# State-space decays from summed logs in a two-layer hybrid block, with their elementwise work moved off GpSimd

## The chip, the cores and the metric

The kernel runs on one core of one Trainium2 chip. The metric is the device time of one execution in microseconds (us); the number compared is the median of several runs. PE is the matrix engine (its weight loads are PEld), DVE the vector engine, ACT the scalar engine, POOL is GpSimd, SP issues the DMAs.

## The reference, cut to what matters

The whole program is a four-part model (two mixers and two expert layers) followed by a second model of two layers. Only the state-space part of those last two layers is touched. Per layer, 256 tokens in two chunks of 128, 32 heads of 64 channels in four groups of eight:

```python
def ssd_scan(xdt, la, bm, cm):          # la = dt * a, the log decay of each token and head
    ...
    def step(state, inp):
        xc, lac, bc, cc = inp
        acs = jnp.cumsum(lac, axis=1)
        seg = acs[:, :, None] - acs[:, None, :]
        lmat = jnp.where(mask, jnp.exp(jnp.where(mask, seg, 0.0)), 0.0)
        cb = jnp.einsum('bign,bjgn->bijg', cc, bc)
        y = jnp.einsum('bijgr,bjgrp->bigrp', cb[..., None] * lmat, xc)
        ...
ys = ys + d_skip * xs
ys = ys * silu(z)
ysg = ysg * rsqrt(mean(ysg * ysg) + EPS)    # one norm for each group of 512 channels
o_ssd = ys @ ssd_out
```

The decay between token j and token i of one head is the exponential of a difference of two running sums of `la`.

## The kernel before, in words

Each layer's matrix products are put in a list, the `Stream`. An item is one 512-column slab of a weight matrix, an item with 1024 rows takes four steps, and one step is one 128x2048 block of fp32 weights: `st.step()` issues the 24 products of a step in two halves of 12. Every weight is split into a high and a low fp32r part, ACT copying the high part (L293) and one engine subtracting it for the low part (L298); three products (L317) then give one fp32-like product. A step needs its own two blocks, split two steps ahead into one of three buffers. The low part runs on DVE, unless `self.on_pool` is 2: then every second one runs on POOL. An item ends with its evacuation: a convolution for the x channels (`conv`, ACT L1882, three DVE operations L1885, ACT L1886), a SiLU for the gate channels z (L1896), a sigmoid for the later gates (L1907).

The small stages are put between the steps by hand, in the order of the code. In `hybrid`, the retention part comes first; the state-space part begins with `st.through(n_ret)`. From there the list holds x0, z0, x1, z1, x2, z2, x3, z3 (four steps each), four gate items, the two slabs of `ssd_out` (eight steps each) and two of `w_o`: 72 steps.

For each group g and each half q (four heads), `decays` makes the matrices S0 (128x1024) and s1 (128x512): `logs` multiplies the causal mask `tri` with the high and the low part of the log decays, the high part on POOL and the low part on DVE (tile latri, L2019); `sums` multiplies these with a matrix of ones or with the strict mask (12 products of 512 columns, L2033), so that each sum of logs is made in the matrix engine; ACT takes exponentials from PSUM (L2039, L2042, L2044); DVE multiplies S0 by the masked scores cb (L2045) and POOL multiplies s1 (L2046). `prepare` runs this for group g+1 while group g is scanned: `tokens` transposes x (L2055) and weights it by dt (L2058), `scan` multiplies (L2069, L2072) and adds the skip (L2075), then ysT is multiplied by the gate (L2133), and `inv_rms` gives the norm: squares on ACT (L1760), two additions on POOL (L1761, L1763), a product with ones (L1767), a power on POOL (L274), a product that spreads it over partitions (L1753). `finish` applies it a group later (L2108, then split L305, L306). `inv_rms` also serves the four retention heads of a layer.

`tc.keep_in_program_order` (`keep`) pins an instruction behind everything written before it for its engine; what is not pinned is ordered by the compiler's own schedule. PSUM is eight banks: four for the stream's products (mm), four for all small stages (sml).

Of the kernel before, what the change touches and what calls it, by code (L numbers as in the profile page):

```python
# [10 lines left out]
F32 = mybir.dt.float32  # L11
F32R = mybir.dt.float32r
I32 = mybir.dt.int32
AF = mybir.ActivationFunctionType
OP = mybir.AluOpType
AX = mybir.AxisListType

T = 256
D = 1024
P = 128  # L20
# [127 lines left out]
class Model:  # L148
# [1607 lines left out]
    def inv_rms(self, yT, n, eps):  # L1756

        nc = self.nc
        sq = self.s("ir_q", [P, 4, T])
        nc.scalar.activation(sq, yT, AF.Square)  # L1760
        nc.gpsimd.tensor_tensor(sq[:, 0:2], sq[:, 0:2], sq[:, 2:4], op=OP.add)  # L1761
        s1 = self.s("ir_s", [P, T])
        nc.gpsimd.tensor_tensor(s1, sq[:, 0], sq[:, 1], op=OP.add)  # L1763
        yield
        pq = self.psum("sml")
        for t in range(2):
            ins = nc.tensor.matmul(pq[:, t:t + 1], s1[:, t * P:(t + 1) * P], self.ones[:, :1], start=t == 0, stop=t == 1)  # L1767
# [5 lines left out]
        pr = self.psum("sml")  # L1773
# [27 lines left out]
    def hybrid(self, l, cc, st, xT, consts=lambda: None):  # L1801
        nc, I = self.nc, self.I
        V, G, A, E = nc.vector, nc.gpsimd, nc.scalar, nc.tensor
        keep = self.tc.keep_in_program_order
# [170 lines left out]
        dtp, la, lar = next(dt)  # L1975
# [11 lines left out]
        tj = next(dt)  # L1987
# [25 lines left out]
        def logs(g, q, c):  # L2013

            h0 = g * 8 + q * 4
            out = []
            for part, eng in ((0, G), (1, V)):
                x_ = self.s("latri", [P, 4, P], F32R)
                eng.tensor_tensor(x_, tri.unsqueeze(1).to_broadcast([P, 4, P]),  # L2019
                                  lar[part][:, c, h0:h0 + 4].bitcast(F32).unsqueeze(2).to_broadcast([P, 4, P]), op=OP.mult)  # L2020
                out.append(x_)
            return out

        def decays(g, q, cb, s1):

            h0 = g * 8 + q * 4
            s0 = self.s("S0", [P, 4, T])
            lt = [logs(g, q, 0), logs(g, q, 1)]

            def sums(m, c, first=False):  # L2030
                p = self.psum("sml")
                for part in range(2):
                    ins = E.matmul(p, self.strict_ones[:, m], lt[c][part], start=part == 0, stop=part == 1)  # L2033
                    if first and part == 0:
                        keep(ins)
                return p
            yield
            p0 = sums(0, 0, True)
            A.activation(s0[:, :, 0:P], p0.rearrange("p (h i) -> p h i", h=4), AF.Exp)  # L2039
            p1 = sums(1, 1)  # L2040
            for j in range(4):
                A.activation(s0[:, j, P:T], p1[:, j * P:(j + 1) * P], AF.Exp, bias=tj[:, h0 + j:h0 + j + 1])  # L2042
            p2 = sums(0, 1)
            A.activation(s1[:, q], p2.rearrange("p (h i) -> p h i", h=4), AF.Exp)  # L2044
            V.tensor_tensor(s0, s0, cb[:, :T].unsqueeze(1).to_broadcast([P, 4, T]), op=OP.mult)  # L2045
            G.tensor_tensor(s1[:, q], s1[:, q], cb[:, T:].unsqueeze(1).to_broadcast([P, 4, P]), op=OP.mult)  # L2046
            yield s0
# [43 lines left out]
        self.on_pool = 2  # L2091
# [21 lines left out]
        for g in range(4):  # L2113
            st.step()
# [8 lines left out]
            st.step()  # L2123
# [4 lines left out]
            st.step()  # L2128
# [16 lines left out]
    def ssd_dt(self, l, cc, xT, sc):  # L2145
# [29 lines left out]
        lar = self.s("la_h", n, F32R), self.s("la_l", n, F32R)  # L2175
        self.split(*lar, la)
        yield dtp, la, lar
        pt = self.psum("sml")
        E.matmul(pt[:, :32], self.masks[:, 1, :], la[:, 0, :], start=True, stop=True)
        tj = self.s("tj", [P, 32])  # L2180
        V.tensor_copy(tj, pt[:, :32])
        yield tj
# [53 lines left out]
    def second_consts(self):  # L2236
# [5 lines left out]
        self.strict_ones = c.tile([P, 2, P], F32R, tag="late", name="strict_ones")  # L2242
        nc.scalar.activation(self.strict_ones[:, 0], self.masks[:, 1], AF.Copy)
        nc.scalar.activation(self.strict_ones[:, 1], self.ones, AF.Copy)
# [178 lines left out]
```

## Time and profile before

| | us |
|---|---|
| median of 3 runs | 2685.36 (2682.80 to 2686.85) |
| the profiled execution | 2682.83 |
| its span, first to last instruction | 2680.7 |
| state-space stage of layer 0, in the span | 1527 to 1692 |
| the same stage of layer 1 | 2220 to 2385 |
| PE busy | 2371.3, 88% of the span |
| DVE busy | 1260.7, 47% |
| ACT busy | 949.0, 35% |
| POOL busy | 492.3, 18% |

The stage of a layer is bounded here by the first product of masked scores (L2005) and the last spread of a norm (L1753). The busy shares are means over stages with different limits, so the stage's own rows count, not the page's.

### The profile page before, as it was taken

To read this page: it belongs to the slowest core of one execution; us is meant where nothing else is said; L and a number is where in the kernel's file an instruction comes from. 1 tells how busy PE (TensorE), PEld (TensorE's weight loads), DVE (VectorE), ACT (ScalarE), POOL (GpSimd) and SP (SyncE) were. 2 spreads that over 40 slices of the span, in tenths; PEclk is the share of its full clock that TensorE was granted. 3 is DMA by queue.
4 is the path that set the end of the run, shared out by engine and by line. 5 is a ranking of instruction groups with operands and counts; after the bars stand their busy time and mean duration, and the time that the engine had idled before them with its cause. 6 is when DMAs were issued, how large, how long until landed. Compare 5 with 4: busy or idle time off the path is not lost.

```text
span 2680.7 us, 40349 instructions
## 1 busy us (share of the span) xinstructions
PE 2371.3 (88%) x16773; PEld 1773.3 (66%) x16773; DVE 1260.7 (47%) x2067; ACT 949.0 (35%) x1565; POOL 492.3 (18%) x426
## 2 busy tenths in 40 slices
PE   8997777776879777777899998999999999899998
PEld 7862222222765222222789988999988999889997
DVE  5751133111863000000657677466556667855664
ACT  6431100001462000000445555454444556554543
POOL 1110001000320000000413165121122305621110
PEclk9998889999889989999999999999999999999999
DMA  5368999999249999999544533555555353344553
GB/s 187 104 258 355 373 421 421 421 421 381 103 137 388 421 421 421 421 422 411 205 167 142 173 127 111 173 173 180 178 180 173 132 184 126 111 157 173 183 188 141
DMA packets 208793, 660.97 MB, mean 247 GB/s; under 512 B 26554, under 2 KB 33116, under 8 KB 161500
## 3 DMA queue, kind: packets, MB, share of 16 engines
q1 hardware_dynamic: 202148, 657.23, 64.4%
q8 instruction: 135, 2.21, 0.3%
q10 hardware_dynamic: 6456, 1.08, 0.2%
q14 instruction: 54, 0.44, 0.0%
HBM read 657.22 MB, written 1.05 MB: 246 GB/s over the span
## 4 chain that ended last, share of the span: by engine, by line
PE 42%; DMA 16%; DVE 5%; POOL 3%; ACT 2%; SPq 1%; issue 1%; POOLq 0%; ACTq 0%; DVEq 0%
PE ps_mm L317 38%; DMA wx<-in_moe_w_down_dram 6%; DMA wx<-in_moe_w_up_dram 5%; DMA wx<-in_moe_w_gate_dram 4%; DVE whl L298 2%; ACT whl L293 1%; DVE cv L1885 1%; DVE latri L2019 1%; PE ps_sml L2069 1%; PE ps_sml L2033 1%; DMA w<-in_w_in_dram 1%; DVE yf L2108 1%; SPq L681 1%; PE ps_sml L1949 1%; POOL xn L1970 0%
## 5 line engine op out<-in xcount | busy, mean ns | idle before, releaser
L317 PE MATMUL ps_mm<-u,whl 128*128 128x256 f32 x8448 | 1058.6, 286 | 24.2 <-POOL whl L298 14.3
L317 PEld LDWEIGHTS ps_mm<-u,whl 128*128 128x128 f32 x8448 | 1035.8, 194 | 37.4 <-POOL whl L298 16.4
L298 DVE TENSOR_TENSOR whl<-w,whl 128x1024 fp32r<-128x1024 f32 x432 | 562.0, 1304 | 425.2 <-ACT whl L293 415.4
L293 ACT ACTIVATE whl<-w 128x1024 fp32r<-128x1024 f32 x472 | 497.1, 1058 | 510.0 <-PE ps_mm L317 479.0
L734 PE MATMUL ps_mm<-wx,xe 128*32 128x512 f32 x2048 | 369.6, 683 | 140.5 <-DMA wx<-in_moe_w_up_dram 93.7
L317 PE MATMUL ps_mm<-whl,u 128*128 128x512 f32 x1440 | 344.3, 396 | 4.8 <-ACT u L305 2.9
L734 PEld LDWEIGHTS ps_mm<-wx,xe 128*32 128x32 f32 x2048 | 81.4, 121 | 402.9 <-DMA wx<-in_moe_w_up_dram 173.2
L317 PEld LDWEIGHTS ps_mm<-whl,u 128*128 128x128 f32 x1440 | 269.6, 190 | 64.6 <-ACT u L305 3.9
L769 PE MATMUL ps_mm<-wx,hid 128*32 128x512 f32 x1024 | 215.8, 608 | 49.7 <-DMA wx<-in_moe_w_down_dram 38.7
L753 DVE TENSOR_TENSOR sl<-sl,ps_mm 128x512 f32<-128x512 f32 x16 | 11.0, 687 | 417.4 <-PE ps_mm L734 342.1
L769 PEld LDWEIGHTS ps_mm<-wx,hid 128*32 128x32 f32 x1024 | 50.8, 110 | 198.3 <-DMA wx<-in_moe_w_down_dram 91.9
L383 POOL TENSOR_TENSOR rstd<-rstd,mhalf 128x1 f32<-128x1 f32 x18 | 10.9, 617 | 795.4 <-DVE rstd L382 786.7
L298 POOL TENSOR_TENSOR whl<-w,whl 128x1024 fp32r<-128x1024 f32 x40 | 97.5, 2439 | 239.4 <-ACT whl L293 239.4
L773 DVE SCALAR_TENSOR_TENSOR y_lo<-ps_mm,sg,y_hi 128x512 fp32r<-128x512 f32 x32 | 24.0, 750 | 233.1 <-ACT y_hi L772 231.8
L760 ACT ACTIVATE hid<-ps_sml 128x512 f32<-128x512 f32 x16 | 9.6, 597 | 311.5 <-PE ps_sml L758 304.0
L772 ACT ACTIVATE y_hi<-ps_mm,sg 128x512 fp32r<-128x512 f32 x32 | 22.0, 688 | 212.4 <-PE ps_mm L769 212.3
L2214 POOL TENSOR_TENSOR yT<-yT,rb 128x256 f32<-128x256 f32 x44 | 40.9, 951 | 204.0 <-ACT yT L2213 204.0
L305 ACT ACTIVATE u<-yf 128x256 fp32r<-128x256 f32 x124 | 48.7, 413 | 72.8 <-DVE yf L2108 21.0
L1885 DVE SCALAR_TENSOR_TENSOR cv<-ps_mm,cols_cw,cv 128x253 f32<-128x253 f32 (+1 forms) x144 | 64.1, 475 | 19.6 <-ACT cv L1882 18.7
L752 ACT ACTIVATE sl<-ps_mm 128x512 f32<-128x512 f32 x16 | 9.6, 597 | 170.7 <-PE ps_mm L734 170.7
L306 DVE TENSOR_TENSOR u<-yf,u 128x256 fp32r<-128x256 f32 x124 | 60.2, 514 | 9.4 <-ACT u L305 9.4
L723 PE MATMUL ps_sml<-oh,u 128*128 128x128 f32 x512 | 62.1, 280 | 2.0 <-ACT u L532 2.0
(518 smaller groups left out, 2160.9 us busy)
## 6 DMA issues: line engine op xcount, KB each, us to landing
wx<-in_moe_w_gate_dram SPq DMA_DIRECT2D x128, 1024.0 KB
wx<-in_moe_w_up_dram SPq DMA_DIRECT2D x128, 1024.0 KB
wx<-in_moe_w_down_dram SPq DMA_DIRECT2D x128, 1024.0 KB
w<-in_w_in_dram SPq DMA_DIRECT2D x104, 1024.0 KB
w<-in_w_gate_up_dram SPq DMA_DIRECT2D x44, 1024.0 KB
w<-in_w_down_dram SPq DMA_DIRECT2D x20, 1024.0 KB
w<-in_ret_out_dram SPq DMA_DIRECT2D x16, 1024.0 KB
w<-in_ssd_out_dram SPq DMA_DIRECT2D x16, 1024.0 KB
```

The costliest lines, as they stand in the source:

```text
L293: ins = nc.scalar.activation(hi, src, AF.Copy)
L298: eng.tensor_tensor(lo, src, hi.bitcast(F32), op=OP.subtract)
L305: self.nc.scalar.activation(hi, src, AF.Copy)
L306: self.nc.vector.tensor_tensor(lo, src, hi.bitcast(F32), op=OP.subtract)
L317: ins = nc.tensor.matmul(out, a, b, start=start and i == 0, stop=stop and i == 2)
L681: nc.sync.dma_start(w, src)
L723: nc.tensor.matmul(pg[:, o:o + P], h[:, t, j, :], oh2[:, t, :], start=j == j0 and t == 0, stop=j == j0 + 3 and t == 1)
L734: nc.tensor.matmul(out[r, :], xe[:, k, r], w[k // 4][a][:, k % 4, :], start=k == 0, stop=k == NK - 1, tile_position=(0, a * SLOTS))
L769: nc.tensor.matmul(py[r, :], hid[:, m, r], wd(c, m, a), start=m == 0, stop=m == 3, tile_position=(0, a * SLOTS))
L1885: V.scalar_tensor_tensor(acc[:, s:], ps[:, :T - s], cw[i][:, b + m:b + m + 1], acc[:, s:], op0=OP.mult, op1=OP.add)
L1949: ins = E.matmul(py[:, o:o + T], v[0, h // 2][:, c0:c0 + P], sc[:, :T], start=b == b0, stop=False, skip_group_check=True)
L2214: nc.gpsimd.tensor_tensor(sil[s0][:, m, :], sil[s0][:, m, :], sc[1], op=OP.mult)
```

## The change

The log decays are summed once per layer, in `ssd_dt`: one product with the causal mask gives the running sums of all 64 columns, they are transposed, and kept as a high and a low row for each head in `rows`. In `decays`, four products per half (64 rows, 256 columns) select a head's row and spread it over all partitions; DVE subtracts the running sum of each partition and clips at zero (eight operations of 128x128 per half), and ACT takes the exponentials from SBUF, pinned to the program's order. The four masked-log products, `logs` and the two POOL multiplications are gone; the additions of `inv_rms` and the s1 product run on DVE; `on_pool` is no longer set in this stage. Three of the single steps in the group loop become two, so a group takes 11 steps instead of 8, and the norm of a group begins one step later after its squares.

```diff
     def inv_rms(self, yT, n, eps):
-        nc.gpsimd.tensor_tensor(sq[:, 0:2], sq[:, 0:2], sq[:, 2:4], op=OP.add)
+        nc.vector.tensor_tensor(sq[:, 0:2], sq[:, 0:2], sq[:, 2:4], op=OP.add)
         s1 = self.s("ir_s", [P, T])
-        nc.gpsimd.tensor_tensor(s1, sq[:, 0], sq[:, 1], op=OP.add)
+        nc.vector.tensor_tensor(s1, sq[:, 0], sq[:, 1], op=OP.add)
...
-        def logs(g, q, c):
...
         def decays(g, q, cb, s1):
             h0 = g * 8 + q * 4
             s0 = self.s("S0", [P, 4, T])
-            lt = [logs(g, q, 0), logs(g, q, 1)]
-
-            def sums(m, c, first=False):
...
+            banks = [self.psum("sml") for _ in range(2)]
+            along = [banks[j // 2][:, j % 2 * T:(j % 2 + 1) * T] for j in range(4)]
+            for j in range(4):
+                ins = E.matmul(along[j], self.heads[0:64, h0 + j:h0 + j + 1].to_broadcast([64, P]), rows, start=j % 2 == 0, stop=j % 2 == 1)
+                if j == 0:
+                    keep(ins)
+            for j in range(4):
+                for c, to in ((0, s0[:, j, 0:P]), (1, s1[:, q, j])):
+                    V.tensor_scalar(to, along[j][:, c * P:(c + 1) * P], sums[:, c, h0 + j:h0 + j + 1], 0.0, op0=OP.subtract, op1=OP.min)
             yield
-            p0 = sums(0, 0, True)
-            A.activation(s0[:, :, 0:P], p0.rearrange("p (h i) -> p h i", h=4), AF.Exp)
-            p1 = sums(1, 1)
             for j in range(4):
-                A.activation(s0[:, j, P:T], p1[:, j * P:(j + 1) * P], AF.Exp, bias=tj[:, h0 + j:h0 + j + 1])
-            p2 = sums(0, 1)
-            A.activation(s1[:, q], p2.rearrange("p (h i) -> p h i", h=4), AF.Exp)
+                keep(A.activation(s0[:, j, P:T], along[j][:, P:T], AF.Exp, bias=tj[:, h0 + j:h0 + j + 1]))
+            keep(A.activation(s0[:, :, 0:P], s0[:, :, 0:P], AF.Exp))
+            keep(A.activation(s1[:, q], s1[:, q], AF.Exp))
             V.tensor_tensor(s0, s0, cb[:, :T].unsqueeze(1).to_broadcast([P, 4, T]), op=OP.mult)
-            G.tensor_tensor(s1[:, q], s1[:, q], cb[:, T:].unsqueeze(1).to_broadcast([P, 4, P]), op=OP.mult)
+            V.tensor_tensor(s1[:, q], s1[:, q], cb[:, T:].unsqueeze(1).to_broadcast([P, 4, P]), op=OP.mult)
             yield s0
...
-        self.on_pool = 2
         pre = prepare(0)
...
         for g in range(4):
-            st.step()
+            st.step(2)
             if last:
                 finish(*last)
...
             ysT = self.u4([P, 4, T], "ys%d" % g)
-            st.step()
+            st.step(2)
             scan(g, 0, s0[0], s1, xdt, xs, ysT)
...
-            st.step()
+            st.step(2)
             scan(g, 1, s0[1], s1, xdt, xs, ysT)
...
     def ssd_dt(self, l, cc, xT, sc):
...
-        lar = self.s("la_h", n, F32R), self.s("la_l", n, F32R)
-        self.split(*lar, la)
-        yield dtp, la, lar
+        yield dtp
         pt = self.psum("sml")
-        E.matmul(pt[:, :32], self.masks[:, 1, :], la[:, 0, :], start=True, stop=True)
+        E.matmul(pt[:, :64], self.masks[:, 0, :], la.rearrange("p c h -> p (c h)"), start=True, stop=True, skip_group_check=True)
+        E.matmul(pt[:, 64:96], self.masks[:, 1, :], la[:, 0, :], start=False, stop=True, skip_group_check=True)
+        sums = self.s("la_sums", [P, 2, 2, 32])
+        for i in range(2):
+            V.tensor_copy(sums[:, :, i], pt[:, :64].rearrange("p (c h) -> p c h", c=2))
         tj = self.s("tj", [P, 32])
-        V.tensor_copy(tj, pt[:, :32])
-        yield tj
+        V.tensor_copy(tj, pt[:, 64:96])
+        pr = self.psum("sml")
+        for c in range(2):
+            E.transpose(pr[0:64, c * P:(c + 1) * P], sums[:, c].rearrange("p i h -> p (i h)"), self.ident)
+        rows = self.s("la_rows", [P, T], F32R)
+        high = self.s("la_high", [P, T], F32R)
+        A.activation(rows[0:32], pr[0:32, :T], AF.Copy)
+        A.activation(high[32:64], pr[32:64, :T], AF.Copy)
+        V.tensor_tensor(rows[32:64], pr[32:64, :T], high[32:64].bitcast(F32), op=OP.subtract)
+        yield sums[:, :, 0], rows[0:64], tj
```

## Rows read from the trace of the kernel before

**Rows 1.** The page's part 1: span, and busy time of each engine.
```profile
span 2680.7 us, 40349 instructions
PE 2371.3 (88%) x16773; PEld 1773.3 (66%) x16773; DVE 1260.7 (47%) x2067; ACT 949.0 (35%) x1565; POOL 492.3 (18%) x426
```

**Rows 2.** Table by stretch: us, busy of PE, PEld, DVE, ACT, POOL, clock, DMA.
```profile
1480.00:1527.00 47.00, 47.00 (x394) 47.00 (x393) 24.90 (x29) 22.73 (x32) 0.00 (x0) 1.00 0.55 187
...
1527.00:1692.00 165.00, 148.98 (x1149) 139.67 (x1148) 124.79 (x160) 94.43 (x166) 97.32 (x55) 0.97 0.35 119
2220.00:2385.00 165.00, 148.99 (x1149) 139.67 (x1148) 124.74 (x160) 94.44 (x166) 97.48 (x55) 0.97 0.35 119
```

**Rows 3.** PE's waits in 1527 to 1692: us in total, times, longest.
```profile
PE ps_mm L317 <- POOL whl L298: 7.2, 5, 1.6
PE ps_sml L2055 <- ACT u L1886: 6.5, 3, 2.4
PE ps_sml L2033 <- DVE latri L2019: 1.0, 2, 0.6
PE ps_sml L1753 <- POOL ir_r L274: 0.8, 1, 0.8
PE ps_sml L2033 <- POOL latri L2019: 0.4, 1, 0.4
```

**Rows 4.** PE in order of time, around one group's decays: start, duration, instruction.
```profile
1603.23 1.65 PE L2033 MATMUL ps_sml<-latri,strict_ones 128*128 128x512 f32 x6
1604.72 3.04 PE L317 MATMUL ps_mm<-u,whl 128*128 128x256 f32 x24
1607.59 1.53 PE L2033 MATMUL ps_sml<-latri,strict_ones 128*128 128x512 f32 x6
1608.96 5.92 PE L317 MATMUL ps_mm<-u,whl 128*128 128x256 f32 x48
1614.72 0.50 PE L1767 MATMUL ps_sml<-c_ones,ir_s 128*128 128x1 f32 x4
```

**Rows 5.** PE in order of time, the first products after three of the waits.
```profile
1578.16 4.39 PE L317 MATMUL ps_mm<-u,whl 128*128 128x256 f32 x22 [1.63 <-POOL whl L298]
...
1591.96 4.61 PE L317 MATMUL ps_mm<-u,whl 128*128 128x256 f32 x24
...
1668.22 4.12 PE L317 MATMUL ps_mm<-u,whl 128*128 128x256 f32 x24
```

**Rows 6.** Table by stretch again, one of those three places (columns of Rows 2).
```profile
1592.00:1597.00 5.00, 5.00 (x32) 4.73 (x31) 3.34 (x6) 2.42 (x6) 0.00 (x0) 0.66 0.37 137
```

**Rows 7.** DVE's groups by shape in 1527 to 1692: busy us, mean ns, idle before.
```profile
L298 DVE TENSOR_TENSOR whl<-w,whl 128x1024 fp32r<-128x1024 f32 x20 | 36.9, 1846 | 17.5 <-ACT whl L293 17.4
L2019 DVE TENSOR_TENSOR latri<-c_masks,la_l 128x512 fp32r<-128x512 f32 x16 | 21.8, 1398 | 0.0
L2045 DVE TENSOR_TENSOR S<-S,cbm 128x1024 f32<-128x1024 f32 x8 | 12.7, 1586 | 5.2 <-ACT S L2042 5.2
L2108 DVE SCALAR_TENSOR_TENSOR yf<-u,cols_b,ir_b 128x256 f32<-128x256 f32 x12 | 11.0, 938 | 0.0
L2133 DVE TENSOR_TENSOR u<-u,u 128x1024 f32<-128x1024 f32 x4 | 8.2, 2040 | 0.0
...
L2008 DVE TENSOR_TENSOR cbm<-ps_sml,c_masks 128x128 f32<-128x128 f32 x4 | 1.2, 292 | 0.7 <-PE ps_sml L2006 0.7
```

**Rows 8.** Single lines, ns min/median/max: L298 in 1480 to 1527, then L2019 and L2108, whole span.
```profile
L298 DVE TENSOR_TENSOR whl<-w,whl x17: 1210/1225/1227, 1479.8 to 1526.5; 128x1024 fp32r<-128x1024 f32 x17
...
L2019 DVE TENSOR_TENSOR latri<-c_masks,la_l x32: 745/1522/2826, 1529.0 to 2335.5; 128x512 fp32r<-128x512 f32 x32
...
L2108 DVE SCALAR_TENSOR_TENSOR yf<-u,cols_b,ir_b x32: 468/472/2601, 1587.1 to 2387.9; 128x256 f32<-128x256 f32 x32
```

**Rows 9.** ACT in order of time: first and last step of one convolution's evacuation (x1).
```profile
1574.19 0.60 ACT L1882 ACTIVATE cv<-ps_mm,cols_b,cols_cw 128x256 f32<-128x256 f32 x1
...
1590.97 0.42 ACT L1886 ACTIVATE u<-cv 128x256 f32<-128x256 f32 x1
```

More of the change, by code (lines that the diff above doesn't have):

```diff
@@ L1974, in hybrid @@
         st.through(n_v - 1)
-        dtp, la, lar = next(dt)
+        dtp = next(dt)
         sc = scores(0)
@@ L1986, in hybrid @@
         sc = scores(1)
-        tj = next(dt)
+        sums, rows, tj = next(dt)
         for h in range(4):
@@ L2011, in masked @@
             return cb
-        def logs(g, q, c):
[L2015 to L2022, printed above, removed]
         def decays(g, q, cb, s1):
@@ L2027, in decays @@
             s0 = self.s("S0", [P, 4, T])
-            lt = [logs(g, q, 0), logs(g, q, 1)]
-            def sums(m, c, first=False):
[L2031 to L2036, printed above, removed]
+            banks = [self.psum("sml") for _ in range(2)]
[7 more added lines that the diff above has]
+                    V.tensor_scalar(to, along[j][:, c * P:(c + 1) * P], sums[:, c, h0 + j:h0 + j + 1], 0.0, op0=OP.subtract, op1=OP.min)
             yield
-            p0 = sums(0, 0, True)
-            A.activation(s0[:, :, 0:P], p0.rearrange("p (h i) -> p h i", h=4), AF.Exp)
-            p1 = sums(1, 1)
             for j in range(4):
-                A.activation(s0[:, j, P:T], p1[:, j * P:(j + 1) * P], AF.Exp, bias=tj[:, h0 + j:h0 + j + 1])
-            p2 = sums(0, 1)
-            A.activation(s1[:, q], p2.rearrange("p (h i) -> p h i", h=4), AF.Exp)
+                keep(A.activation(s0[:, j, P:T], along[j][:, P:T], AF.Exp, bias=tj[:, h0 + j:h0 + j + 1]))
+            keep(A.activation(s0[:, :, 0:P], s0[:, :, 0:P], AF.Exp))
+            keep(A.activation(s1[:, q], s1[:, q], AF.Exp))
             V.tensor_tensor(s0, s0, cb[:, :T].unsqueeze(1).to_broadcast([P, 4, T]), op=OP.mult)
-            G.tensor_tensor(s1[:, q], s1[:, q], cb[:, T:].unsqueeze(1).to_broadcast([P, 4, P]), op=OP.mult)
+            V.tensor_tensor(s1[:, q], s1[:, q], cb[:, T:].unsqueeze(1).to_broadcast([P, 4, P]), op=OP.mult)
             yield s0
@@ L2241, in second_consts @@
         self.retm = self.retm.rearrange("p (h t) -> p h t", h=4)
-        self.strict_ones = c.tile([P, 2, P], F32R, tag="late", name="strict_ones")
-        nc.scalar.activation(self.strict_ones[:, 0], self.masks[:, 1], AF.Copy)
-        nc.scalar.activation(self.strict_ones[:, 1], self.ones, AF.Copy)
+        self.heads = c.tile([P, 32], F32R, tag="late", name="heads")
+        for i in range(2):
+            nc.scalar.activation(self.heads[32 * i:32 * i + 32], self.ident[32 * i:32 * i + 32, 32 * i:32 * i + 32], AF.Copy)
         cc = {}
```

## The prediction
> **What bounds the kernel now.** The page comes first: PE is busy for 88% of the span, DVE for 47%, POOL for 18% [rows 1]. Those are means, so I went next to the table by stretch. Just ahead of the state-space stage PE is busy without a gap (47.00 of 47.00 us) with POOL at zero; inside the stage it is busy 148.98 of 165 us in one layer and 148.99 in the other, with POOL at 97 and DVE at 125 [rows 2]. The two layers repeat to 0.1 us, so I work out one and double it. PE is the bound, and what the change can give is (a) PE work taken away, (b) PE's idle time, (c) what PE loses at a lower clock. The list of PE's waits names (b): 7.2 us for low weight parts made on POOL, 6.5 us for the SiLU of a convolution that is late when `tokens` wants it, 1.4 us for latri, 0.8 us for the power of a norm: 15.9 us, the whole gap [rows 3]. [...]
>
> Why are the waits there? DVE's groups show it. A 128x1024 split takes 1.225 us on DVE while POOL is idle and 1.846 us on average in the stage [rows 7, 8]. The same holds for the norm products L2108 (0.938 against 0.47), L2045 and L2133. Taken at undisturbed lengths (1.225 for 128x1024, 0.47 for L2108), the four groups would need 24.5 + 5.6 + 9.8 + 4.9 us instead of 36.9 + 11.0 + 12.7 + 8.2: 24 of DVE's 125 us are stretch from work beside POOL. A convolution's evacuation therefore lasts from 1574.19 to 1591.39, 17.2 us [rows 9], and `tokens` waits for its end.
>
> **The change part by part, for one layer, then doubled.** All is set against the profiled execution, 2682.83 us: the span of 2680.7 and 2.1 around it. The median of the runs is 2.5 us higher and the forecast is given for it.
>
> PE work. Two batches of six L2033 and one step fill 1603.23 to 1608.96, 5.73 us; two steps fill 1608.96 to 1614.72, so a step is 2.88, and a product of 512 columns is 2.85/12 = 0.2375 us, one of 256 columns 2.88/24 = 0.12 us [rows 4]. Removed: 48 x 0.2375 = 11.4. Added: 32 selecting products of 256 columns. They have half the rows and a repeated weight column, which the trace doesn't show; 0.12 (a 256-column product) is the nearest row, 0.2375 the upper bound, and fewer rows give no reason for less than 0.12. I take 0.12: 3.8 us (7.6 at the bound). Net -7.6, both layers -15.1 (-7.6 at the bound).
>
> Waits removed. With no latri, no POOL split and more steps between a group's parts, every row of [rows 3] loses its cause. x1 ends at step 12; `tokens(1)` stood at step 16 and now stands at step 20, `tokens(2)` moves from 24 to 31 with x2 done at 20. That is 8 to 11 steps (23 us or more) against a chain of 17.2. The norm's squares get three steps (8.6 us) before L1767 instead of two. Sum -15.9, both layers -31.8. The slow products after those waits go with them: 4.39, 4.61 and 4.12 against 2.8 (for 22), 3.04 and 3.04, together 4.2; both layers -8.4 to -8.6.
>
> So if nothing new were late, the change would bring 15.1 + 31.8 + 8.5 = 55 us.
>
> DVE's load. This is what the new waits come from. Within the 39 steps that the stage holds now: 125 us, less the stretch (24), less latri (21.8) leaves 79. Added: 19 splits that POOL made, 19 x 1.225 = 23.3; eight s1 products of 128x512 at latri's shortest 0.745, 6.0; the norm's two additions four times, at 0.745 and 0.47, 4.9; 64 subtractions of 128x128 from PSUM at 0.29, 18.6, from the mask product of that shape [rows 7, 8]. Together 132 us. DVE is thus as loaded as before, but nobody shares the work. Because a group now takes 11 steps, 13 further steps (37 us of PE, 16 of DVE) come into the stage: 148 us of DVE against PE's 165 - 15.9 - 4.2 - 7.6 + 37 = 174. Over the whole stage that is 85%. It isn't even: three of the four convolutions end in the first 24 steps, where by the same prices DVE has about 75 to 80 us of work to PE's 76; group 3 has no convolution and no decays. In the first two groups DVE is nearly the bound.
>
> [...]
>
> New waits. Three places, each with what queues behind it. First, sml has four banks and the two halves hold two each from the selecting products to the exponentials: the second half's second bank comes free only when DVE has read the bank of `scan` (L2075) or ACT has taken half 0's exponentials. The first of those products is pinned, and the next step's first product is pinned behind them, so PE waits with the whole stream behind it. In group 0, x1 ends one step earlier, so DVE has 12 convolution operations (5.7), two splits (2.45) and the two L2075 (0.95) to do in the time of one step and a scan (2.88 + 1.5): 4.7 us late. In groups 1 and 2 it is about 1 us each. Second, DVE's lag in steps 4 to 26: if it keeps busy for 90% of that time it falls some 7 us behind, and the two steps of look-ahead take back about 3.5: 4 us on PE. Third, the exponentials are pinned on ACT behind everything written before them; what is queued behind is the next high part, with the same two steps of cover. I put that at nothing here and price it as a rival. Together 11 us per layer, 22 in all; bounds are 4 per layer (banks only, shorter chain) and 20 per layer, today's 15.9 waits + 4.2 slow products, DVE being no less loaded than now.
>
> The log sums. Per layer PE gets two more passes of the small product and two transposes; four small passes take 0.50 [rows 4], so 0.5 us, and the transposes wait for DVE to copy the sums, with the norm's product and the next step pinned behind them: one undisturbed split ahead on DVE is 1.2 us. 1.7 per layer, 3.4 in all; bounds 0.5 and 3 per layer. The ACT copies and the subtraction that follow are not wanted until the state-space stage; they cost nothing, and 1 us at most if that cover goes. The additions moved from POOL to DVE in the retention heads (1.2 us for each head) sit two steps or more ahead of their product while DVE is idle for half of the time (24.90 of 47 busy in the stretch without POOL [rows 2]): nothing, at most 1 us. `heads` instead of `strict_ones` happens once, under the earlier part: nothing.
>
> **Sum.** -55 + 22 + 3.4 = -30: profiled 2653, median 2655.
>
> **The rivals.** *DVE takes PE's place as the bound.* If DVE stays busy for only 85% in the first 37 steps (it is at 125/165 = 76% today), its 125 us there last 147 against PE's 128: about 20 us per layer. Then -55 + 40 + 3.4 = -12, 2673. For: DVE's idle before single operations [rows 7] (17.5 us for ACT's high parts, 5.2 for exponentials) isn't removed. Against: most DVE work now has several steps of room, only splits are urgent.
>
> *The waits go and nothing replaces them.* New waits of 4 per layer: -55 + 8 + 1.5 = -45, 2640.
>
> *Pinned exponentials block ACT: slower.* The convolution's SiLU waits on DVE; an exponential pinned behind it waits as well, and the next high parts, if the schedule leaves them behind it, wait with them. If the chain stays at 17.2 us at three convolutions per layer, less two steps of cover (5.8), it costs 11.4 x 6 = 68 us: -55 + 68 + 3.4 = +16, 2702. It decides from a chain of about 14.5 us. For: today's chain is longer. Against: its stretch came from POOL, undisturbed it is 12 x 0.475 and some splits, 10 us; and only x1 ends right before an exponential.
>
> *No change.* The new waits are as large as the old (20 per layer and the price of the selecting products at its bound): -55 + 40 + 7.5 + 3.4 = -4, 2681.
>
> **How the numbers follow.** The forecast -30 (gains of 20 to 38) gets 0.53; DVE as the bound 0.19; nothing replaces the waits 0.10; no change 0.08; slower by blocked ACT 0.10. The predicted time is that of the forecast, 2655. The range leaves out the slower rival and the farthest ends of the neighbours: 2634 (hardly a new wait at all, no cost of the log sums) to 2681 (the no-change case). About 0.2%, 5.4 us, is what a measurement of this kernel can tell from no change. Faster by more: 0.53 + 0.19 + 0.10 = 0.82; within: 0.08; slower by more: 0.10.
>
> **What would show it.** In the profile after, the stage from the first L2005 to the last L1753 of a layer should be near 185 to 190 us for 51 steps (202 would be no gain: 164.5 now and 13 steps of 2.88). PE's waits for POOL splits, latri and the late SiLU should be gone, and PE's waits should name the low parts on DVE and the sml banks of the selecting products instead, about 10 us in a layer. DVE's splits should all be near 1.225 us and L2108 near 0.47. The selecting products should follow each other at 0.12 us; 0.2 or more makes the first term wrong. The forecast is wrong towards slower if ACT idles in front of the exponentials while high parts stand behind them; it is wrong towards faster if PE's waits in the stage sum to under 5 us.

## The result, and the profile after

The changed kernel takes 2654.91 us, median of 5 runs (2652.86 to 2656.07), against 2683.54 us (2682.30 to 2686.85) before: a ratio of 0.9892, 95% interval 0.9881 to 0.9902. The forecast was 2655. The total came out; the reasons did so only in part. First the page, part 1, then the table by stretch (columns as in [rows 2]): the stretch ahead of layer 0's state-space stage, and the stage of layer 0 and of layer 1.

```profile
span 2653.6 us, 40343 instructions
PE 2366.9 (89%) x16749; PEld 1766.2 (67%) x16749; DVE 1268.8 (48%) x2253; ACT 970.1 (37%) x1581; POOL 281.8 (11%) x308
```

```profile
1490.00:1536.00 46.00, 46.00 (x385) 46.00 (x385) 23.80 (x29) 22.73 (x32) 0.00 (x0) 1.00 0.53 182
1536.70:1716.70 180.00, 173.98 (x1419) 166.73 (x1418) 140.30 (x254) 120.22 (x197) 5.39 (x5) 0.99 0.42 144
2211.60:2392.30 180.70, 175.17 (x1419) 167.83 (x1418) 140.33 (x254) 120.12 (x197) 5.40 (x5) 0.98 0.42 143
```

POOL falls from 97 to 5 us in the stage [rows 2]; PE idles 6 us instead of 16. From the first L2005 to the last L1753 layer 0 now takes 179.8 us, and it holds 49 steps instead of 37 (1176 products of the stream instead of 888, 24 a step). With the 12 added steps at 2.88 us the old 164.5 would be 199.1: the stage gained 19.3 us, and in layer 1 18.5 (164.6 + 34.6 - 180.7).

PE's waits in the stage of layer 0 (us in total, times, longest), to be laid beside [rows 3]:

```profile
PE ps_mm L317 <- ACT whl L293: 3.0, 1, 3.0
PE ps_mm L317 <- DVE whl L298: 1.6, 3, 0.9
PE ps_sml L1753 <- POOL ir_r L274: 0.7, 1, 0.7
PE ps_sml L2021 <- DVE u L2062: 0.6, 1, 0.6
```

None of the old waits is left but the norm's power. The largest new one is a single wait for a *high* part on ACT, which the forecast had at nothing. DVE's groups by shape (busy us, mean ns, idle before), beside [rows 7]:

```profile
L298 DVE TENSOR_TENSOR whl<-w,whl 128x1024 fp32r<-128x1024 f32 x50 | 60.5, 1220 | 20.4 <-ACT whl L293 20.4
L2026 DVE TENSOR_SCALAR S<-ps_sml,la_sums 128x128 f32<-128x128 f32 x32 | 10.9, 342 | 0.3 <-PE ps_sml L2021 0.3
...
L2032 DVE TENSOR_TENSOR S<-S,cbm 128x1024 f32<-128x1024 f32 x8 | 9.8, 1224 | 7.8 <-ACT S L2030 7.8
...
L2094 DVE SCALAR_TENSOR_TENSOR yf<-u,cols_b,ir_b 128x256 f32<-128x256 f32 x12 | 5.2, 478 | 1.8 <-ACT ir_b L1776 1.8
```

Every DVE operation shown is back at its undisturbed length: 1.220 us for a split that took 1.846, 0.478 for a norm product that took 0.938 [rows 7, 8].

**Where the 27 us of the span are.** I cut it at the first product of the `dt` turn, the first instruction of the second model that the change can reach. Before, it starts at 1378.40 us, after at 1386.40: the first block, in which the change touches nothing but the two copies that fill `heads`, became 8.0 us *longer*. From there to the end it was 1302.3 us and is now 1267.2: 35.1 us less (two stages 37.8, the log sums cost 1.2 a layer). So 27 = 35 - 8, and both parts need a cause.

### The profile page after: what moved, and what is told of

The parts are those of the page before. It is cut to its first block, busy times and chain, and to the rows that moved or that the text cites. A ratio compares the mean times of both kernels' runs of the same rounds, so it can differ in the third digit from the quotient of the medians.

```text
span 2653.6 us, 40343 instructions
## 1 busy us (share of the span) xinstructions
PE 2366.9 (89%) x16749; PEld 1766.2 (67%) x16749; DVE 1268.8 (48%) x2253; ACT 970.1 (37%) x1581; POOL 281.8 (11%) x308
## 4 chain that ended last, share of the span: by engine, by line
PE 43%; DMA 15%; ACT 3%; DVE 2%; POOL 2%; issue 2%; SPq 1%; POOLq 0%; ACTq 0%; DVEq 0%
PE ps_mm L317 38%; DMA wx<-in_moe_w_up_dram 5%; DMA wx<-in_moe_w_down_dram 5%; DMA wx<-in_moe_w_gate_dram 4%; DVE whl L298 1%; ACT whl L293 1%; SPq L681 1%; PE ps_sml L2056 1%; PE ps_sml L1949 1%; PE ps_mm L769 1%; POOL xn L1970 0%; POOL yf L1921 0%; PE ps_sml L2021 0%; POOL yf L1920 0%; ACT L1886 0%
## 5 line engine op out<-in xcount | busy, mean ns | idle before, releaser
L298 DVE TENSOR_TENSOR whl<-w,whl 128x1024 fp32r<-128x1024 f32 x470 | 581.3, 1242 | 383.6 <-ACT whl L293 382.0
L734 PE MATMUL ps_mm<-wx,xe 128*32 128x512 f32 x2048 | 377.6, 696 | 140.3 <-DMA wx<-in_moe_w_up_dram 93.0
L274 POOL TENSOR_TENSOR ir_r<-rs_t,mhalf 128x2 f32<-128x2 f32 x16 | 13.5, 842 | 614.5 <-DVE rs_t L272 614.5
L1885 DVE SCALAR_TENSOR_TENSOR cv<-ps_mm,cols_cw,cv 128x253 f32<-128x253 f32 (+1 forms) x144 | 64.1, 477 | 7.4 <-ACT cv L1882 6.7
L723 PEld LDWEIGHTS ps_sml<-oh,u 128*128 128x128 f32 x512 | 60.7, 198 | 5.4 <-DVE x L412 2.9
```

The source lines that it names most:

```text
L298: eng.tensor_tensor(lo, src, hi.bitcast(F32), op=OP.subtract)
L723: nc.tensor.matmul(pg[:, o:o + P], h[:, t, j, :], oh2[:, t, :], start=j == j0 and t == 0, stop=j == j0 + 3 and t == 1)
L734: nc.tensor.matmul(out[r, :], xe[:, k, r], w[k // 4][a][:, k % 4, :], start=k == 0, stop=k == NK - 1, tile_position=(0, a * SLOTS))
L1885: V.scalar_tensor_tensor(acc[:, s:], ps[:, :T - s], cw[i][:, b + m:b + m + 1], acc[:, s:], op0=OP.mult, op1=OP.add)
```

## The experiments

All kernels in one table, each timed against the kernel before. "Second block" is from the first `dt` product to the span's end; "stage" is layer 0's, first L2005 to last L1753, and for kernels with 11 steps a group the 34.6 us of the 12 added steps are taken off, so that the column can be compared down its length; "waits" are PE's idle time in that stage.

| kernel | median us | ratio, 95% interval | first `dt` product | second block | stage | waits |
|---|---|---|---|---|---|---|
| before | 2683.5 | | 1378.4 | 1302.3 | 164.5 | 15.9 |
| after | 2654.9 | 0.9892, 0.9881 to 0.9902 | 1386.4 | 1267.2 | 145.2 | 5.9 |
| after_again | 2652.3 | 0.9884, 0.9861 to 0.9906 | 1384.1 | 1267.2 | 145.2 | 5.9 |
| pool_splits_back | 2661.7 | 0.9916, 0.9893 to 0.9939 | 1387.7 | 1274.8 | 149.6 | 7.8 |
| eight_steps | 2689.6 | 1.0019, 1.0010 to 1.0029 | 1385.9 | 1302.6 | 162.6 | 17.1 |
| old_decays | 2653.2 | 0.9893, 0.9866 to 0.9919 | 1378.6 | 1271.1 | 149.1 | 5.3 |
| only_eleven | 2662.3 | 0.9924, 0.9903 to 0.9945 | 1380.0 | 1280.9 | 153.4 | 9.3 |
| only_pool_off | 2646.8 | 0.9866, 0.9846 to 0.9886 | 1377.8 | 1265.6 | 146.1 | 1.7 |
| silu_first | 2654.2 | 0.9894, 0.9874 to 0.9914 | 1383.5 | 1267.0 | 145.4 | 5.4 |
| no_pins | 2659.6 | 0.9915, 0.9894 to 0.9936 | 1386.1 | 1271.8 | 148.7 | 7.5 |
| eight_no_pins | 2680.5 | 0.9989, 0.9979 to 0.9998 | 1384.5 | 1293.7 | 159.0 | 13.0 |
| padded_heads | 2648.5 | 0.9872, 0.9855 to 0.9888 | 1381.5 | 1265.8 | 144.8 | 5.7 |
| decays_alone | 2706.5 | 1.0086, 1.0069 to 1.0103 | 1382.0 | 1324.9 | 175.5 | 22.7 |
| shifted | 2653.3 | 0.9890, 0.9873 to 0.9906 | 1385.7 | 1265.7 | 146.1 | 1.6 |

**The change as it is, once more** (after_again), for the size of what is only spread.

> The changed kernel once more, unaltered. In its first profile the code ahead of the second block, which the change doesn't touch, ended 8.0 us later than in the profile of before (the first product that turns dt at 1386.4 us against 1378.4). If that is chance of one execution, it lies elsewhere here, between 1378 and 1386, and the span ends accordingly at 2646 to 2654; if the change does it (other addresses of the code, another schedule), it lies at 1386 again. Either way the stage of a layer should be 180 us again, with PE's waits summing to about 6 us.

Measured: 2652.3 us. The second block repeats to 0.1 us; the first differs by 2.3 us, so a first block alone tells little below that.

**POOL's splits back in the changed kernel** (pool_splits_back).

```
+        self.on_pool = 2
         pre = prepare(0)
```

> The changed kernel with every second low part on POOL again, nothing else. My theory (POOL's work beside DVE stretches DVE, and low parts of 2.4 us on POOL are late): DVE's splits go from 1.22 us back towards 1.5, PE's waits for low parts on POOL return with 3 to 6 us a layer, 2660 to 2668. The rival that DVE is the bound of the changed kernel: relieved of some 25 splits (30 us a layer) it lets PE's waits for DVE go, 2648 or less.

Measured: second block 1274.8, 7.6 us more. The waits and the splits on DVE:

```profile
PE ps_mm L317 <- POOL whl L298: 3.6, 2, 1.9
PE ps_mm L317 <- ACT whl L293: 1.8, 3, 1.2
```

```profile
L298 DVE TENSOR_TENSOR whl<-w,whl 128x1024 fp32r<-128x1024 f32 x25 | 35.1, 1405 | 18.5 <-ACT whl L293 18.5
```

PE waits for POOL's low parts again, and the splits left on DVE take 1.405 instead of 1.220 us. With 11 steps of room this costs 4 us a layer. What the same line costs in the kernel before is the next question.

**POOL's splits away in the kernel before, and nothing else** (only_pool_off).

```
-        self.on_pool = 2
         pre = prepare(0)
```

> The kernel before with on_pool at zero and nothing else: old decays, 8 steps a group. My theory of the prediction had POOL's splits as a cause that stands by itself: their 7.2 us a layer and half of the slow products go, 2660 to 2668. The theory after the last four runs, that eight steps leave the convolution no room whoever does the splits: the late SiLU takes over, 2678 to 2690.

Measured: 2646.8 us, the fastest median of all, below both ranges expected and 5 to 8 us below the whole change. The stage's waits, then its groups of splits and latri on DVE:

```profile
PE ps_sml L1753 <- POOL ir_r L274: 0.9, 3, 0.3
PE ps_sml L2055 <- ACT u L1886: 0.8, 3, 0.3
```

```profile
L298 DVE TENSOR_TENSOR whl<-w,whl 128x1024 fp32r<-128x1024 f32 x38 | 51.8, 1371 | 16.8 <-ACT whl L293 16.8
...
L2019 DVE TENSOR_TENSOR latri<-c_masks,la_l 128x512 fp32r<-128x512 f32 x16 | 10.6, 695 | 0.1
```

One line took away 14.2 of the 15.9 us of waits: the late SiLU (6.5 us in [rows 3], 0.8 here) and the latri waits were not causes of their own but effects of the splits on POOL. latri halves from 1.398 to 0.695 us though POOL still makes its high half; the splits are still stretched (1.371), and no wait for one is left.

How a split on POOL reaches the SiLU can be read in the kernel before, in the convolution of [rows 9] (start, duration):

```profile
1575.77 3.42 DVE L298 TENSOR_TENSOR whl<-w,whl 128x1024 fp32r<-128x1024 f32 x1
1575.77 2.33 POOL L298 TENSOR_TENSOR whl<-w,whl 128x1024 fp32r<-128x1024 f32 x1
```

Two splits start together and DVE's takes 3.42 us; the next tap of the convolution (L1885, 0.47 us) stands behind it until 1579.11. The evacuation lasts 17.2 us here and 14.5 in only_pool_off (1569.30 to 1583.79). No run separates this stretch from the length of POOL's own splits (2.45 us against 1.22), which stands behind the 7.2 us of waits for low parts.

**The change without its new decays** (old_decays: only_pool_off with the step counts of the change), **and the step counts alone** (only_eleven, on the kernel before).

```
-            st.step()
+            st.step(2)
```
(at the three places of the group loop that the change's diff shows)

> The kernel before with on_pool left at zero and 11 steps a group, its own decays, its norm additions on POOL. My theory: the 12 products of 512 columns are back in place of 8 of 256 columns (+6.1 us of PE a layer), the log sums are cheaper by 1.2 us a layer, latri (24 us on POOL, 22 on DVE) stretches DVE's work, 3 to 5 us of waits a layer more: 2670 to 2675. The rival, that all of the gain is in the schedule (splits off POOL and more steps) and the new sums of logs only move work: 2655 to 2660.

> The kernel before with 11 steps a group and nothing else: old decays, every second low part on POOL. If room alone is the cause of the gain, it comes out at the 2653 of the kernel that also has POOL off. If POOL's low parts have their own share, PE's waits for them stay (7.2 us a layer before, 3.6 in the changed kernel with POOL splits back), the SiLU that tokens waits for is in time: 2660 to 2666.

Measured: 2653.2 us, below both ranges expected, and 2662.3, within the second. Without the new decays the change has the same median: its second block is 3.9 us longer, its first 5.5 to 7.8 us shorter (more on that below). Room alone brings 21 us of second block, by outlasting most of POOL's delays; once these are gone, 11 steps *cost* the old decays 5.5 us of second block (1271.1 against 1265.6). The waits of old_decays name the cost, one high part that is late:

```profile
PE ps_mm L317 <- ACT whl L293: 3.6, 1, 3.6
```

**The change with 8 steps a group** (eight_steps: the diff above, undone).

> The changed kernel with single steps in the group loop again (8 steps a group in place of 11). If the room between the parts of a group carries a share of the gain, DVE has some 125 us of work in the time of 139 us of PE, the SiLU that tokens waits for is late again by 1 to 2 us a group, low parts are late: 15 us of waits a layer, 2670 to 2675. The rival, that taking POOL out is what counts and the steps are along for the ride: waits stay near 6 us a layer, 2655 to 2659.

Measured: 2689.6 us, slower than either theory had it, the whole gain gone. PE's waits in the stage are one row, and ACT's order shows where (start, duration):

```profile
PE ps_sml L2042 <- ACT u L1886: 17.1, 10, 3.0
```

```profile
1582.78 1.04 ACT L1760 ACTIVATE ir_q<-u 128x1024 f32<-128x1024 f32 x1
1583.73 1.13 ACT L2029 ACTIVATE S<-ps_sml,tj 128x128 f32<-128x128 f32 x4
1584.73 0.65 ACT L2030 ACTIVATE S<-S 128x512 f32<-128x512 f32 x1
1585.25 0.65 ACT L2031 ACTIVATE u<-u 128x512 f32<-128x512 f32 x1
1585.77 1.08 ACT L293 ACTIVATE whl<-w 128x1024 fp32r<-128x1024 f32 x1
1586.71 0.58 ACT L1882 ACTIVATE cv<-ps_mm,cols_b,cols_cw 128x256 f32<-128x256 f32 x1
...
1599.83 0.42 ACT L1886 ACTIVATE u<-cv 128x256 f32<-128x256 f32 x1
```

The convolution's first step (L1882) stands behind a norm's squares and the exponentials pinned after them; its last SiLU comes at 1599.83, and `tokens` waits. How much of it is the pins' the next run tells.

**8 steps, and the exponentials not pinned** (eight_no_pins).

```
-                keep(A.activation(s0[:, j, P:T], along[j][:, P:T], AF.Exp, bias=...))
+                A.activation(s0[:, j, P:T], along[j][:, P:T], AF.Exp, bias=...)
```
(and the other two exponentials likewise)

> The changed kernel with 8 steps a group, as before, and with the exponentials no longer tied to the place in ScalarE's order at which they are written. Theory A (at 8 steps the pins hold the convolution's SiLUs behind exponentials that stand behind the norm's Square, and TensorE waits 17 us a layer for the last SiLU): the waits of the tokens' products for the SiLU fall under 6 us a layer and the time comes to about 2655 to 2665 us, against 2689.6 with the pins. Theory B (8 steps are simply too short a cover for the new decays' chain of products, VectorE subtractions, exponentials and VectorE products, wherever the exponentials stand): the waits stay over 12 us a layer, under another name or the same, and the time at 2680 to 2695 us.

Measured: 1293.7 us of second block, 8.9 below eight_steps and 28 above only_pool_off; the SiLU's wait falls from 17.1 to 9.9 us. So it is mostly theory B, by the time and by 13.0 us of waits in all: the pins are a quarter of the loss, and the rest comes with the new decays at 8 steps, with POOL's work on DVE.

**The new decays alone, with POOL's part as before** (decays_alone: eight_no_pins with three operations back on POOL, and `heads` padded as below).

```
-        nc.vector.tensor_tensor(sq[:, 0:2], sq[:, 0:2], sq[:, 2:4], op=OP.add)
+        nc.gpsimd.tensor_tensor(sq[:, 0:2], sq[:, 0:2], sq[:, 2:4], op=OP.add)
```
(so also the second addition of `inv_rms` and the s1 product)

> The kernel before without GpSimd's low parts, as only_pool_off, and with the new decays on top, and nothing else: 8 steps a group, the norm's sums and the second product by cb on GpSimd as before, the exponentials not tied in ScalarE's order, the table of the selecting columns padded to the old size. Against only_pool_off (2646.8 us) TensorE has about 6 us less work a layer. Theory A (at 8 steps the new decays stall because VectorE also got the norm's sums and the second product, 10 us a layer that stand ahead of the convolution's taps): the wait for the SiLU falls under 3 us a layer and the time comes to 2637 to 2646 us, the best of all. Theory B (the subtractions and the later exponentials alone delay the convolution, whose taps and SiLUs share VectorE and ScalarE with them): the wait stays at 6 to 10 us a layer and the time at 2655 to 2672 us.

Measured: 2706.5 us, slower than either theory. PE's waits, then POOL's costliest group:

```profile
PE ps_sml L2042 <- ACT u L1886: 11.9, 4, 3.9
PE ps_sml L1767 <- POOL ir_s L1763: 10.5, 3, 3.5
```

```profile
L2033 POOL TENSOR_TENSOR u<-u,cbm 128x512 f32<-128x512 f32 x8 | 20.0, 2499 | 173.2 <-ACT u L2031 173.2
```

Taking 10 us of work off DVE did not bring the SiLU forward, so that work alone does not explain the delay. The test is not clean: with POOL beside it the S0 product on DVE takes 1.45 us instead of 1.22, and PE has a new wait. What stays as suspect is the 64 subtractions and the later exponentials; no run here takes these alone away. And on POOL the s1 product takes 2.50 us (0.68 on DVE) and waits for its exponentials, the last ones of a half, with the norm's additions behind it in POOL's queue: PE waits 10.5 us for these. So at 8 steps moving the rest of POOL's work to DVE is right *for the new decays* (31 us of second block against eight_no_pins); with the old decays POOL keeps it and PE waits 1.7 us (only_pool_off).

**Other orders of the exponentials at 11 steps.** The wait for a high part in the changed kernel is in group 0, where ACT does this (start, duration):

```profile
1592.08 1.28 ACT L1886 ACT_TABLE_LOAD   x1
1593.38 0.42 ACT L1886 ACTIVATE u<-cv 128x256 f32<-128x256 f32 x1
1593.80 1.28 ACT L2029 ACT_TABLE_LOAD   x1
1595.10 0.89 ACT L2029 ACTIVATE S<-ps_sml,tj 128x128 f32<-128x128 f32 x3
1595.86 0.64 ACT L2030 ACTIVATE S<-S 128x512 f32<-128x512 f32 x1
1596.38 0.64 ACT L2031 ACTIVATE u<-u 128x512 f32<-128x512 f32 x1
1597.04 1.28 ACT L1896 ACT_TABLE_LOAD   x1
1598.33 1.21 ACT L1896 ACTIVATE u<-ps_mm 128x256 f32<-128x256 f32 x4
1599.40 2.02 ACT L293 ACTIVATE whl<-w 128x1024 fp32r<-128x1024 f32 x2
```

Exponentials and SiLUs alternate and each switch loads a table, 1.28 us; 16 loads in the stage where there were 9. The high part of the next step is made last, and PE stands:

```profile
1596.94 0.60 PE L1753 MATMUL ps_sml<-c_ident,ir_r 128*128 128x128 f32 x4
1600.54 0.74 PE L317 MATMUL ps_mm<-u,whl 128*128 128x256 f32 x4 [2.99 <-ACT whl L293]
1601.80 7.02 PE L317 MATMUL ps_mm<-u,whl 128*128 128x256 f32 x44 [0.52 <-DVE whl L298]
```

The 44 products behind it take 7.02 us where 44 at 0.12 take 5.28; the granted clock of that stretch is 0.76 (0.50 from 1603 to 1606, 1.00 from 1607), after PE had stood for 2.99 us.

The place comes with the 11 steps, not with the new decays or the pins: old_decays, which has neither, shows the same wait (3.6 us, above) in the same group, behind the same turns of SiLUs and exponentials. It loads 14 tables in its stage, and so does only_eleven; every kernel with 8 steps loads 9, with either decays. Two edits try other orders: silu_first issues a half's exponentials after the last SiLU of the convolution written before them; no_pins lets the schedule place them.

```
-            keep(A.activation(s0[:, :, 0:P], s0[:, :, 0:P], AF.Exp))
+            with self.tc.issue_after(self.silu.ins):
+                A.activation(s0[:, :, 0:P], s0[:, :, 0:P], AF.Exp)
```
(silu_first, for all the exponentials of a half; no_pins as in eight_no_pins, with 11 steps)

> The changed kernel with its exponentials queued behind the last SiLU of the convolution written before them, instead of behind ACT's previous instruction. In group 0 ACT now alternates between the two tables (16 loads in a layer's stage, 9 before). If that is what makes PE wait 3.0 us for a high part and then run slowly, there are about 10 loads, that wait goes with 1.5 to 3 us of slow products behind it: 5 us a layer, 2641 to 2646. If the wait comes from the amount of work at that place, it stays or moves to the low parts on DVE: 2650 to 2656.

> The changed kernel with its exponentials not pinned at all. If the pins do nothing at 11 steps a group (each ties an exponential only to the one ACT instruction written before it), the order on ACT is the same or nearly so: 2650 to 2656. If they are what keeps the exponentials together, ACT loads tables more often than 16 times a layer and 2660 or more follows.

Measured: second blocks of 1267.0 and 1271.8 us against 1267.2. The order of silu_first shortens the wait for high parts to 1.2 us and gets another of 1.7, which the trace puts down to an exponential; without pins the wait for high parts grows to 4.3. The pins are worth 4.6 us at 11 steps, and at 8 they cost 8.9.

**The first block.** Some 5 to 9 us turned up in every kernel with the new decays and in none with the old. The one thing there that the change alters is a size: `heads` takes 128 bytes a partition where `strict_ones` took 1024, and the next largest tile of that place has 896. So the place shrinks, and every tile behind it moves down by 128 bytes, among them the buffers into which the expert weights stream. Two runs test this from both sides: the changed kernel with `heads` at the old size, and the fastest kernel with its tiles moved up by 384 bytes, the same place within 512.

```
-        self.heads = c.tile([P, 32], F32R, tag="late", name="heads")
+        self.heads = c.tile([P, 2 * P], F32R, tag="late", name="heads")[:, 0:32]
```
(padded_heads)

> The changed kernel with one edit that computes nothing: the table of the selecting columns gets the 1024 bytes a partition that the two matrices before had, of which only the first 128 are used, so every tile behind it in the scratchpad stands at the byte address that it has in the kernel before. Theory A (the first block, which the change does not touch, is slower after because all later tiles stand 128 bytes lower): the dt turn's first product comes at about 1378.5 us of the trace instead of 1384 to 1386, the second block stays at 1267, and the time is about 2646 us, near 0.986 of before. Theory B (the first block's 5 to 9 us have another cause, such as the order in which the instructions stand, or the spread between chips): the first product stays at 1384 to 1386 and the time at 2652 to 2655 us.

```
-        self.strict_ones = c.tile([P, 2, P], F32R, tag="late", name="strict_ones")
+        self.strict_ones = c.tile([P, 2 * P + 96], F32R, tag="late", name="strict_ones")[:, 0:2 * P].rearrange("p (m k) -> p m k", m=2)
```
(shifted, on only_pool_off)

> The best kernel so far (the one before without GpSimd's low parts, 2646.8 us) with 384 unused bytes a partition behind the two matrices of the old decays, so that every tile behind them stands 384 bytes higher: within each 512 bytes that is the place that these tiles have in the changed kernel. No instruction changes. Theory A (the place of the tiles within 512 bytes slows the streams of the first block): the expert stage from its first gathering product near 865 us to the first transpose near 1277 us takes 413 to 415 us instead of 411.1 to 411.5, the first dt product comes 2 to 6 us later than 1377.8 us, the second block keeps its 1265.6 us, and the time is 2649 to 2653 us. Theory B (the place does nothing; the new decays' kernels lose it in another way, and the padded one gained by chance): 411.1 to 411.5 us, 1377 to 1380 us, and 2645 to 2648 us.

PE in order of time: the start of the last seven expert groups, the first transpose after them, the first `dt` product; only_pool_off first, then shifted.

```profile
865.16 3.82 PE L723 MATMUL ps_sml<-oh,u 128*128 128x128 f32 x32
1276.40 1.25 PE L455 MATMUL ps_sml<-c_ident,x 128*128 128x128 f32 x8 [0.31 <-DVE x L412]
1377.76 0.63 PE L2160 MATMUL ps_sml<-c_ident,dt_t 32*128 32x32 f32 x4 [0.52 <-ACT dt_t L2157]
```

```profile
870.09 3.82 PE L723 MATMUL ps_sml<-oh,u 128*128 128x128 f32 x32
1284.62 1.25 PE L455 MATMUL ps_sml<-c_ident,x 128*128 128x128 f32 x8 [0.31 <-DVE x L412]
1385.67 0.63 PE L2160 MATMUL ps_sml<-c_ident,dt_t 32*128 32x32 f32 x4 [0.52 <-ACT dt_t L2157]
```

Same instructions, other addresses: 1385.67 instead of 1377.76, a second block equal to 0.1 us, and 6.5 us in the median (on two chips, whose medians of the kernel before are 3.2 us apart). The expert stretch between the first two rows takes 411.2 us in one and 414.5 in the other. Over all kernels it takes 411.1 to 411.5 us in the six at the old addresses (padded_heads and decays_alone among them) and 412.8 to 414.7 in the eight at the other place; no value lies between. The order of the first block's instructions is no rival: on every engine, DMA issues included, it is the same in all fourteen traces, but for four neighbouring products in two of them. The rates of 925 to 1225 us agree (last column GB/s; only_pool_off, then shifted):

```profile
925.00:1225.00 300.00, 232.70 (x1215) 74.18 (x1214) 27.73 (x62) 18.84 (x30) 0.00 (x0) 0.94 1.01 421
```

```profile
925.00:1225.00 300.00, 231.14 (x1210) 74.54 (x1207) 27.49 (x61) 18.83 (x30) 0.00 (x0) 0.94 1.01 419
```

The padding gave the changed kernel back its expert stretch (411.3 us) and 3.8 to 6.4 us in the median. It didn't give back all: its first `dt` product is at 1381.5 where the old decays have 1377.8 to 1380.0. These 1.5 to 3.7 us lie in small pieces ahead of 865 us, of the size by which after and after_again differ there; their cause stays open.

So the place of the tiles is shown as the cause of 1.2 to 3.6 us in the expert stretch. In the changed kernel's own profile that stretch holds only 1.5 of the 8.0 us (412.9 against 411.4). The other 6.6 lie ahead of it (872.2 against 865.7), where the kernels at the two places overlap (865.2 to 869.6 and 867.8 to 872.2); for that part no run gives a cause.

## Why the prediction was right, and where not

**What bounds the kernel: right.** PE was the bound, its waits in the stage were the money, and DVE's stretch beside POOL was behind them.

**PE work: right in kind, 1.5 us a layer too good.** The selecting products follow each other at 0.165 us (four from 1571.67 to 1572.32, the next step's product behind them), between the 0.12 I took and the 0.2375 of the upper bound: 5.3 us a layer instead of 3.8. The term is -6.1, not -7.6.

**Waits removed: right in sum, wrong in attribution.** I gave "every row of [rows 3] loses its cause" to no latri, no POOL split *and* more steps together, and set the SiLU's 6.5 us against the room of 11 steps. only_pool_off shows the POOL splits as the cause of 14.2 of 15.9 us. The chain was in the prediction (stretch, then a late evacuation, then `tokens`), but its three cures were priced as one; I did not ask what the cheapest gives alone, and it gives nearly all.

**New waits: 5.9 and 5.3 us a layer, not 11**, inside the bounds of 4 to 20. The place was wrong. The sml bank of group 0, which I had at 4.7 us, cost 0.6; DVE's lag, 4 us, came to 1.6. The 3.0 us are ACT's, which I had put at nothing: I read `keep` as holding an exponential behind *everything* written before it, whereas in the trace exponentials and a convolution's SiLUs alternate, with a table load of 1.28 us at each turn. That they meet there comes with the 11 steps (old_decays), so my room had a price of its own. With these waits smaller, the stage gained more than the sign I had named: 19.3 and 18.5 us, where 185 to 190 against 202 meant 12 to 17.

**Slow products: 5 us in all, not 8.5.** The 8.5 are the places of [rows 5] against the step of [rows 4], in both layers. Beyond waits and PE work the stages gained 3.2 and 1.8 us, an estimate of this term; the new waits have slow products of their own. The second block then adds up: 12.2 of PE work, 20.6 of waits and 5.0, less 2.4 for the log sums, is 35.4, and 35.1 were measured.

**DVE's load: 140 us, not 148.** Undisturbed, its operations came as forecast (1.220, 0.478). The s1 product took 0.684 where I took 0.745. A subtraction lasts 0.342, not 0.29, but the next starts 0.26 after it, as here:

```profile
1573.03 0.34 DVE L2026 TENSOR_SCALAR S<-ps_sml,la_sums 128x128 f32<-128x128 f32 x1
1573.29 0.34 DVE L2026 TENSOR_SCALAR u<-ps_sml,la_sums 128x128 f32<-128x128 f32 x1
```

So 64 of them occupy an estimated 16.6 us (64 x 0.26), not 18.6.

**The count of steps.** I counted 13 steps into the stage and 51 in all; the trace has 12 more, and 49 in all by its products. Both sides of the comparison shift by 2.88 us, and the gain doesn't.

**Log sums: 1.2 us a layer against 1.7.** PE waits 0.70 us for DVE's copies ahead of the transposes, as described.

**The part not foreseen: the first block.** "`heads` instead of `strict_ones` happens once, under the earlier part: nothing" is the step that failed by most: 8.0 us in the profiled execution, 5.7 in the second one; the padded kernel gives about half back. The second block gained 35 us where I had 30, and the two errors nearly cancel. A forecast that hits by a cancellation has not been shown right by its total.

**The rivals.** *Pinned exponentials block ACT* is real, at 8 steps: the late SiLU came back with 17.1 us a layer, though only 4.5 us a layer of the loss are the pins'. The chain of 10 us that I set against it was too short: in only_pool_off, without POOL's splits, it is 14.5. At 11 steps no wait for a SiLU is left, so it is the room that keeps this rival away. *DVE as the bound* did not come about: 140 of 180 us, and 1.6 us of waits. *Nothing replaces the waits* is what only_pool_off does, which gets 1265.6 with none of the change's other parts.

**What the parts are worth, then.** POOL's splits away: 36.7 us of second block. The new decays at 8 steps, unpinned and with DVE doing POOL's work: +28.1; there PE waits 9.9 us a layer for the convolution's SiLU. 11 steps and the pins: -26.5, which repairs that. In sum the other parts come to +1.6 us (+0.2 with `heads` padded, 1265.8), and the size of `heads` costs some 4 to 6 more in the median: the kernel before without one line beats the whole change. With 11 steps on both sides the new decays, with POOL's work moved to DVE, do gain: 3.9 us of second block (1271.1 to 1267.2), or 5.3 with `heads` padded, a third to a half of the 11.7 that their PE work and log sums promised.

## What to carry to other kernels

When one engine's work stretches another's (here a split from 1.220 to 1.846 us), take that contention away first and alone, and look again: the waits further down the chain may be its effects, and parts that were meant to cure them may then only cost. A new scheme that lengthens a chain has to be tried at the old spacing too, or the added room is credited to it; and the old scheme at the new spacing, since room can have its own price (here a wait of 3.6 us in old_decays). When a change alters the size of a tile that lives as long as the kernel, pad it to the old size before comparing (here 3.8 to 6.4 us in the median), and compare the parts of the trace whose code didn't change.

## What the runs showed of the hardware

**DVE beside POOL.** In the stage of the kernel before, the 6 recorded splits on DVE that no POOL instruction overlaps take 1.22 us on average, the 13 that one overlaps 2.19 (up to 3.42). Both inputs of a split lie in SBUF, as do those of four others that stretch too [rows 7]: L2045 takes 1.21 us where no POOL instruction overlaps it and 1.81 where one does, L2108 0.47 and 2.34, L2133 1.22 and 2.31; the 16 latri are all overlapped and take 1.398, where in only_pool_off they take 0.695. The convolution's taps (L1885), which read one input from PSUM, don't: 0.475 us for the 26 that POOL overlaps and 0.474 for the other 22.

**The place of a DMA's target.** The place of the streamed weight buffers within 512 bytes moved the expert stretch, in which the DMA share is 1.01 (925 to 1225 us), by 0.3 to 0.9% (411.1 to 411.5 us against 412.8 to 414.7; 421 against 419 to 420 GB/s). Among the eight kernels at the worse place, the changed kernel has 412.8 and 412.9 us in its two profiles and the other six kernels 414.5 to 414.7; what parts these is not known. Only two places were tried: the changed kernel and shifted have the buffers at the same offset within 512 bytes; which offsets are good was not tried. The second block, where the DMA engines are busy for under half of the time (0.46 before, 0.47 after), showed no difference in one pair (only_pool_off 1265.6, shifted 1265.7 us) and 1.4 us in the other (padded_heads 1265.8, after 1267.2).
